# Raising the priority of the output projections' additions in VectorE's order, in a four-layer hybrid kernel on one core

## Chip, core and metric

The kernel runs on one NeuronCore of one Trainium2 chip. The metric is the device time of one execution in microseconds (us); smaller is better. A run is one timed execution; the time of a kernel is the median of its runs. Beside the timed runs one execution was recorded by the hardware profiler, and all rows of the profile come from that one.

## The reference

The reference takes a sequence of 1024 tokens of width 1024, puts 16 learned "meta" tokens in front (1040 tokens that count), and sends them through four layers. Each layer normalises the residual stream, projects it to the inputs of a mixer, runs the mixer, gates its output, projects that back to width 1024 and adds it to the residual stream:

```python
h = concat(padding, meta, x)
for i in range(4):
    u = rmsnorm(h, norm_gain[i])
    if i % 3 == 0:   y = attention_branch(u, ...)   # layers 0 and 3: sliding window, 16 heads, 4 kv heads
    elif i % 3 == 1: y = mlstm_branch(u, ...)       # layer 1: 8 heads, 128 keys, 256 values
    else:            y = hgrn2_branch(u, ...)       # layer 2: 8 heads, 128 by 128
    h = h + where(valid, y, 0)
return h[:, first_real_token:]

# the end of each branch, for instance attention
return (o * silu(z)).astype(u.dtype) @ w_out
```

The last line, the output projection, and the addition `h + y` are what the change is about. All in float32.

## The kernel before

**Layout.** The residual stream `x` stands in SBUF, transposed: 8 tiles of 128 channels (index `m`) by 1040 tokens. Tokens are worked on in three chunks of 400, 384 and 256 columns (`CHUNKS`; the last layer leaves the 16 meta tokens out and has 384, 384 and 256). Every large product is made of three matmuls, since each float32 operand is split into a high part and a remainder, `h` and `l` (`split`, lines 194 to 196: a copy on ScalarE, a subtraction on VectorE): high by high, high by low, low by high.

**Output projection** (`proj_out`, line 297). It takes two 128-row pieces of a mixer's gated output at a time (two heads' worth in attention and in the third kind of layer, one head's in the second kind) and adds their product with the output weights into `x`. For each chunk, `ysplit` (line 310) splits the two pieces into `yh` and `yl`; then for each of the 8 channel tiles `m` and the two pieces `k`, `product` (line 318) issues three matmuls into one PSUM tile `acc` (line 326). When `k` is 1 the sum is whole, and line 329 adds it on VectorE from PSUM into `x`. Below, this instruction is called an **x-addition**. There are 8 for each chunk and 480 in all: 192 in the two attention layers, 192 in the second layer, 96 in the third. After a layer's last projection `fin` runs behind each x-addition: the square of `x` on ScalarE and its addition on VectorE for the next layer's normalisation (`Norm.sq`, lines 351 and 355), or the store of the result in the last layer.

**PSUM.** All PSUM tiles, whatever they are for, come from one pool of 8 buffers of one bank each (`psum`, line 147). The names tell their use: `pj` projections (the input projections of line 231 and 281 and the output projection), `pm`, `pt`, `po`, `pa` the mixers' scores, transposes, outputs and sums. A tile is free again when the last engine has read it; for an output projection that is the x-addition.

**Order of the work.** TensorE's order is written out by hand: the body of each layer is a list of steps with costs (`[cost, function, prefetch]`), woven from the mixers' steps and filling work by their costs (`weave`, line 58), and TensorE runs what the steps issue in that very order (`manual_schedule`, line 118). The weights of a step are loaded and split some 12 us of step cost ahead (`LOOKAHEAD`, line 1503). The orders on VectorE, ScalarE, GpSimd and the DMA queue are made when the program is built: a planner goes through the program on a clock of its own, and whenever an engine is free it takes, of the instructions that are ready by that clock, the one with the smallest priority number. The number is the instruction's place in the order in which the program was written out. On the chip each engine then works through its fixed list. `hi` lowers the number by 40 places for what a function issues:

```python
PRIO = 40
def hi(fn):
    def f():
        with tc.high_priority(offset=PRIO):
            fn()
    return f
```

Before the change, `hi` is put around the mixers' steps and around `ysplit`. In attention the mixers' steps are `S_step` (line 701: scores; on VectorE the masked row minimum L734 and the reciprocal L739, on ScalarE the exponential L737, on GpSimd the scaling L740), `T_step` (line 743: TensorE transposes L755, a copy L757 and a subtraction L758) and `V_step` (line 760: product with the values L773, a copy L781 and an addition L782). One unit is one block of 128 queries for two heads. A unit's transposes come two units behind its scores, and its product with the values four units behind.

Not under `hi` are the x-additions, the rotary embedding of queries (L625 to L627), the split of queries (L528), the gates (L457, L473 to L476), the splits of weights (`wl`, L196), the normalisation of the next layer (`Norm.unit`, L373 and its split `ul`, L196) and the sums of squares (L355).

**Where output projections stand.** In layer 0 the first of the four projections is woven into the mixers (about 153 to 187 us of the profiled execution), the second too (321 to 362), and the last two form the layer's end, with the normalisation for the next layer beside them (428 to 477). Layer 3 has the same plan (2285 to 2317, 2443 to 2486, and the end of the kernel from 2546). Layer 1 has six projections between its heads (from 641 to 1328) and two at its end (1500 to 1549); layer 2 has two among its mixers (1825 to 1855, 1972 to 2003) and two at its end (2103 to 2152).

Of the kernel before, what the change touches and what calls it, by code (L numbers as in the profile page):

```python
# [12 lines left out]
ALU = mybir.AluOpType  # L13
# [100 lines left out]
def hybrid_kernel(ctx: ExitStack, tc: tile.TileContext, ins, out, layers=(0, 1, 2, 3)):  # L114
    nc = tc.nc
    v, s, g, pe, sp = nc.vector, nc.scalar, nc.gpsimd, nc.tensor, nc.sync
# [11 lines left out]
    def nm(x):  # L128
        ctr[0] += 1
        return f"{x}{ctr[0]}"  # L130
# [19 lines left out]
    def psj():  # L150
        return psum("pj", 3)
# [15 lines left out]
    x = cpool.tile([P, KT, T], F32, name="x")  # L167
# [26 lines left out]
    def split(src, h, l):  # L194
        s.copy(h, src)  # L195
        v.tensor_tensor(l, src, h.bitcast(F32), op=ALU.subtract)  # L196

    def weights(src, kind, inrow=False):
        width = src.shape[-1]
        if inrow:  # L200
            h, l = (rrow()[:, :1024] for _ in range(2))
        else:
            h = wpool.tile([P, 1024], F32R, tag="wh", name=nm("wh"), bufs=3)
            l = wpool.tile([P, 1024], F32R, tag="wl", name=nm("wl"), bufs=3)
        for z in (slice(0, width // 2), slice(width // 2, width)):
            raw = wpool.tile([P, 512], F32, tag="raw", name=nm("wr"), bufs=RAWS)[:, : width // 2]
            sp.dma_start(raw, src[:, z])
            split(raw, h[:, z], l[:, z])
        c = dict(m=128, v=256, o=512, g=272)[kind]
        return tuple(z[:, :width].rearrange("p (k c) -> p k c", c=c) for z in (h, l))  # L210
# [79 lines left out]
# [7 lines that stand above are left out]
    def proj_out(src0, src1, y, chunks=CHUNKS, fin=None, inrow=False):  # L297
        st = {}

        def pre0():  # L300
            st[0] = weights(src0, "o", inrow=inrow)

        def pre1():
            st[1] = weights(src1, "o", inrow=inrow)

        groups = []
        for n, (c0, cn) in enumerate(chunks):
            grp = []

            def ysplit(k, n=n, c0=c0, cn=cn):  # L310
                def fn():
                    yh, yl = (tpool.tile([P, 400], F32R, tag=z, name=nm(z), bufs=YS)[:, :cn] for z in ("yh", "yl"))
                    split(y(k)[:, c0 : c0 + cn], yh, yl)
                    st["y", n, k] = yh, yl

                return [0.0, hi(fn), None]

            def product(m, k, n=n, c0=c0, cn=cn):
                h, l = st[m // 4]
                mc = slice((m % 4) * P, (m % 4 + 1) * P)  # L320
                if k == 0:
                    st["p", n, m] = psj()
                acc = st["p", n, m]
                yh, yl = st["y", n, k]
                for i, (a, b) in enumerate(((h, yh), (h, yl), (l, yh))):
                    pe.matmul(acc[:, :cn], a[:, k, mc], b,  # L326
                              start=(k == 0 and i == 0), stop=(k == 1 and i == 2))
                if k == 1:
                    v.tensor_tensor(x[:, m, c0 : c0 + cn], x[:, m, c0 : c0 + cn], acc[:, :cn], op=ALU.add)  # L329
                    if fin:  # L330
                        fin(m, n, c0, cn)

            order = [(m, k) for m in range(KT - Y_LAST) for k in range(2)]
            order += [(m, k) for k in range(2) for m in range(KT - Y_LAST, KT)]
            for m, k in order:
                pre = (pre0, pre1)[m // 4] if (n == 0 and m % 4 == 0 and k == 0) else None
                grp.append([3 * cn * MM, lambda m=m, k=k, product=product: product(m, k), pre])
            groups.append(([ysplit(0), ysplit(1)], grp))
        return groups
# [1103 lines left out]
    for pos, i in enumerate(layers):  # L1443
# [3 lines left out]
        def fin(m, n, c0, cn, nxt=nxt):  # L1447
            if nxt is not None:
                nxt.sq(m, n, c0, cn)
            else:  # L1450
                lo = max(c0, NMETA)
                sp.dma_start(out[m, :, lo - NMETA : c0 + cn - NMETA], x[:, m, lo : c0 + cn])
# [169 lines left out]
```

## Time and profile before

| what | value |
|---|---|
| median of 3 runs | 2601.44 us |
| the 3 runs | 2598.78 to 2603.09 us |
| the profiled execution | 2596.91 us |
| its span, first to last instruction | 2595.1 us |
| granted TensorE clock, mean | 0.999 |
| TensorE busy | 2547.2 us, 98% |
| VectorE busy | 1960.2 us, 76% |
| ScalarE busy | 1689.9 us, 65% |
| GpSimd busy | 245.6 us, 9% |

In the profile PE is TensorE's matmuls, PEld its weight loads, DVE VectorE, ACT ScalarE and POOL GpSimd. L329 is line 329 of the kernel; a helper's line, such as L196, stands for all who call it, and is told apart by the tile that it writes. `x<-x,pj` is an instruction that writes `x` and reads `x` and `pj`. A row of the view of waits reads: who waited, on whom, us in total, how many times, the longest. A row of the timeline reads: start in us, duration in us, engine, line, operation, tiles, shapes, how many; in brackets how long the engine had been idle before it, and whose end released it. A row of the view by stretches gives the stretch and its length, then busy time of PE, PEld, DVE, ACT and POOL.

### The profile page before, as it was taken

The numbers are of one execution on the slowest core, as the hardware profiler recorded it, in microseconds if no ns is written. First come the engines' busy times: TensorE is split into PE (matmuls) and PEld (weight loads), VectorE is DVE, ScalarE is ACT, GpSimd is POOL, SyncE is SP. The second block draws the span as 40 slices with busy tenths as digits, with TensorE's granted clock in tenths as the row PEclk, the third lists the DMA queues.
The fourth block names the chain that finished last, engine by engine and source line by source line (L and its number), as shares of the span: only waits on it lengthen the run. The fifth ranks groups of instructions, "written<-read, shape, count | busy, mean of one in ns | idle before, by whom it ended". The sixth has DMA issues, their size and how long they took to land.

```text
span 2595.1 us, 54389 instructions
## 1 busy us (share of the span) xinstructions
PE 2547.2 (98%) x20446; PEld 2486.5 (96%) x20446; DVE 1960.2 (76%) x5290; ACT 1689.9 (65%) x4434; POOL 245.6 (9%) x564
## 2 busy tenths in 40 slices
PE   8999999999999999999999999999999999999999
PEld 8899999999999999999999999999999999999999
DVE  7897898775656564747474688988888978887996
ACT  8766766666464645555555757877676857767772
POOL 0321231000000000000000000010000000321330
PEclk9999999999999999999999999999999999999999
DMA  5223212021111111111111111111111113212112
GB/s 157 62 66 93 59 43 69 30 67 56 44 54 46 50 49 51 42 58 41 51 46 52 51 34 34 34 35 34 38 39 34 34 51 91 62 44 85 56 42 78
DMA packets 86058, 140.21 MB, mean 54 GB/s; under 512 B 12425, under 2 KB 39186, under 8 KB 85794
## 3 DMA queue, kind: packets, MB, share of 16 engines
q1 hardware_dynamic: 85794, 136.73, 17.1%
q8 instruction: 161, 2.64, 0.4%
q14 instruction: 103, 0.84, 0.1%
HBM read 121.83 MB, written 4.27 MB: 49 GB/s over the span
## 4 chain that ended last, share of the span: by engine, by line
PE 65%; DVE 13%; ACT 9%; issue 2%; DMA 2%; POOL 0%; SPq 0%; DVEq 0%; ACTq 0%; POOLq 0%
PE pj L231 29%; PE pj L326 15%; PE pj L281 10%; DVE wl L196 1%; ACT Sm L737 1%; PE po L1019 1%; PE po L1021 1%; PE pa L1035 1%; DVE Sm L734 1%; PE po L773 1%; ACT wh L195 1%; PE pt L755 1%; ACT X L1249 1%; PE pj L277 1%; DVE t L457 1%
## 5 line engine op out<-in xcount | busy, mean ns | idle before, releaser
L231 PE MATMUL pj<-uh,wh 128*128 128x256 f32 (+2 forms) x2688 | 914.8, 340 | 6.9 <-ACT uh L401 6.4
L231 PE MATMUL pj<-ul,wh 128*128 128x256 f32 (+2 forms) x2688 | 864.2, 322 | 0.3
L231 PE MATMUL pj<-uh,wl 128*128 128x256 f32 (+2 forms) x2688 | 864.3, 322 | 0.0
L231 PEld LDWEIGHTS pj<-uh,wh 128*128 128x128 f32 x2688 | 507.4, 189 | 16.3 <-ACT uh L401 6.4
L231 PEld LDWEIGHTS pj<-ul,wh 128*128 128x128 f32 x2688 | 507.9, 189 | 6.4 <-DVE ul L196 0.9
L231 PEld LDWEIGHTS pj<-uh,wl 128*128 128x128 f32 x2688 | 507.2, 189 | 0.0
L196 DVE TENSOR_TENSOR wl<-wr,wh 128x512 fp32r<-128x512 f32 (+1 forms) x338 | 234.7, 703 | 52.0 <-ACT wh L195 49.3
L195 ACT CAST wh<-wr 128x512 fp32r<-128x512 f32 (+1 forms) x338 | 202.9, 613 | 103.6 <-PE pj L326 32.7
L326 PE MATMUL pj<-yh,wh 128*128 128x384 f32 (+2 forms) x768 | 253.2, 330 | 9.8 <-DVE x L329 8.3
L329 DVE TENSOR_TENSOR x<-x,pj 128x384 f32<-128x384 f32 (+2 forms) x480 | 234.7, 509 | 32.8 <-PE pj L326 31.6
L326 PE MATMUL pj<-yl,wh 128*128 128x384 f32 (+2 forms) x768 | 245.8, 320 | 0.0
L326 PE MATMUL pj<-yh,wl 128*128 128x384 f32 (+2 forms) x768 | 245.8, 320 | 0.0
L281 PE MATMUL pj<-wh,uh 128*128 128x256 f32 (+1 forms) x768 | 232.7, 303 | 0.0
L281 PE MATMUL pj<-wl,uh 128*128 128x256 f32 (+1 forms) x768 | 216.4, 282 | 0.0
L281 PE MATMUL pj<-wh,ul 128*128 128x256 f32 (+1 forms) x768 | 215.9, 281 | 0.0
L737 ACT ACTIVATE Sm<-Sm,s 128x257 f32<-128x257 f32 (+2 forms) x272 | 131.1, 483 | 88.4 <-DVE s L734 85.9
L740 POOL TENSOR_TENSOR Sm<-Sm,s 128x512 f32<-128x512 f32 (+2 forms) x136 | 139.3, 1024 | 403.5 <-DVE s L739 383.3
L458 ACT ACTIVATE t<-t 128x384 f32<-128x384 f32 (+2 forms) x240 | 117.9, 491 | 76.5 <-DVE t L457 75.0
L326 PEld LDWEIGHTS pj<-yh,wh 128*128 128x128 f32 x768 | 144.5, 188 | 14.0 <-DVE x L329 10.4
L195 ACT CAST yh<-r 128x384 fp32r<-128x384 f32 (+2 forms) x120 | 57.0, 479 | 152.0 <-PE pj L326 136.3
L457 DVE SCALAR_TENSOR_TENSOR t<-pj,t 128x400 f32<-128x400 f32 (+2 forms) x168 | 86.5, 515 | 81.6 <-ACT t L456 80.3
L281 PEld LDWEIGHTS pj<-wh,uh 128*128 128x128 f32 x768 | 144.7, 188 | 2.2
(296 smaller groups left out, 5468.3 us busy)
## 6 DMA issues: line engine op xcount, KB each, us to landing
wr<-in_b_win SPq DMA_DIRECT2D x124, 256.0 KB, 2.8
wr<-in_a_win SPq DMA_DIRECT2D x80, 256.0 KB, 2.8
wr<-in_c_win SPq DMA_DIRECT2D x64, 256.0 KB, 2.8
wr<-in_a_wout SPq DMA_DIRECT2D x32, 256.0 KB, 3.0
wr<-in_b_wout SPq DMA_DIRECT2D x32, 256.0 KB, 2.7
t<-t SPq DMA_DIRECT2D x100, 48.0 KB, 1.9
cs<-in_rope SPq DMA_DIRECT2D x11, 400.0 KB, 3.6
cs<-in_rope SPq DMA_DIRECT2D x11, 384.0 KB, 3.5
```

The costliest lines, as they stand in the source:

```text
L195: s.copy(h, src)
L196: v.tensor_tensor(l, src, h.bitcast(F32), op=ALU.subtract)
L231: pe.matmul(acc[:, :cn], a[:, k, :], b[:, k, c0 : c0 + cn], start=(k == 0 and i == 0), stop=(k == KT - 1 and i == 2))
L277: pe.matmul(acc[:48, :nc], um[0][:, k, :], m[:, kk, :], start=(k == 0 and m is wh), stop=(k == KT - 1 and m is wl))
L281: pe.matmul(acc[:cn, :nc], a[:, k, c0 : c0 + cn], m[:, kk, :], start=(k == 0 and j == 0), stop=(k == KT - 1 and j == 2))
L326: pe.matmul(acc[:, :cn], a[:, k, mc], b, start=(k == 0 and i == 0), stop=(k == 1 and i == 2))
L329: v.tensor_tensor(x[:, m, c0 : c0 + cn], x[:, m, c0 : c0 + cn], acc[:, :cn], op=ALU.add)
L457: v.scalar_tensor_tensor(a[:, :cn], z, 0.0, a[:, :cn], op0=ALU.min, op1=ALU.subtract)
L458: s.activation(a[:, :cn], a[:, :cn], AF.Exp)
L734: v.tensor_tensor_reduce(Sm[:nq, u, :nk], S[:nq, u, :nk], R["masks"][:nq, P + mo : P + mo + nk], rq, sinks[u], ALU.add, ALU.min, st[:nq, u ...
L737: s.activation(Sm[:nq, u, : nk + 1], Sm[:nq, u, : nk + 1], AF.Exp, scale=-1.0, bias=st[:nq, u : u + 1], accum_out=den[:nq, u : u + 1])
L740: g.tensor_tensor(Sm[:nq, :, :nk], Sm[:nq, :, :nk], den[:nq].rearrange("p (u c) -> p u c", c=1).to_broadcast([nq, 2, nk]), op=ALU.mult)
```

## The change

Line 329 is issued under `hi`. The priority number of each of the 480 x-additions falls by 40 places. Nothing else is edited; `fin`, which follows, stays as it was. `hi` gives back a function that runs its argument with the lower number, so the call at the end of the new line runs it at once.

```diff
                 if k == 1:
-                    v.tensor_tensor(x[:, m, c0 : c0 + cn], x[:, m, c0 : c0 + cn], acc[:, :cn], op=ALU.add)
+                    xs = x[:, m, c0 : c0 + cn]
+                    hi(lambda: v.tensor_tensor(xs, xs, acc[:, :cn], op=ALU.add))()
                     if fin:
                         fin(m, n, c0, cn)
```

## Prediction

> **What bounds the kernel now.** I read the page's first part, then TensorE's waits, then the stretches in which x-additions run, then the timeline at two stalls.
>
> ```profile
> span 2595.1 us, 54389 instructions
> PE 2547.2 (98%) x20446; PEld 2486.5 (96%) x20446; DVE 1960.2 (76%) x5290; ACT 1689.9 (65%) x4434; POOL 245.6 (9%) x564
> ```
>
> TensorE is busy 98% of the span, so only its 2595.1 - 2547.2 = 47.9 us of idle time are to be had by another order of VectorE's work. The waits say how much of that hangs on x-additions.
>
> ```profile
> engine line waited for: us in total, times, longest us
> PE pt L755 <- POOL Sm L740: 10.7, 10, 2.2
> PE pj L326 <- DVE x L329: 8.3, 7, 2.2
> ...
> PE pm L726 <- DVE x L329: 1.9, 2, 1.7
> ```
>
> 8.3 + 1.9 = 10.2 us: TensorE wants a PSUM bank, for the next projection or for scores, whose x-addition has not run. By place:
>
> ```profile
> PE pj L326 <- DVE x L329: 2.1, 3, 1.6
> ...
> PE pm L726 <- DVE x L329: 1.7, 1, 1.7
> ```
> ```profile
> PE pj L326 <- DVE x L329: 4.0, 3, 1.4
> ```
> ```profile
> PE pj L326 <- DVE x L329: 2.2, 1, 2.2
> ...
> PE pj L231 <- ACT uh L195: 0.5, 1, 0.5
> ...
> PE pm L726 <- DVE x L329: 0.2, 1, 0.2
> ```
>
> These are three answers of the same view, for 153 to 362, 428 to 2160 and 2160 us to the end. Between attention's mixers TensorE loses 2.1 + 1.7 + 2.2 + 0.2 = 6.2 us; at the ends of layers 0, 1 and 2 (428 to 2160) it loses 4.0. Now how full the engines are there:
>
> ```profile
> core 0: us, PE busy (x) PEld busy (x) DVE busy (x) ACT busy (x) POOL busy (x), PEclk, DMA share, GB/s
> 153.00:187.00 34.00, 33.24 (x226) 31.87 (x225) 33.39 (x86) 18.84 (x52) 9.45 (x13) 1.00 0.13 37
> 320.00:362.00 42.00, 38.29 (x272) 36.33 (x272) 40.02 (x120) 26.16 (x86) 12.24 (x27) 1.00 0.14 44
> ...
> 1500.00:1549.00 49.00, 47.56 (x299) 46.92 (x297) 43.57 (x93) 22.13 (x46) 0.84 (x3) 1.00 0.07 22
> ...
> 1972.00:2003.00 31.00, 31.00 (x413) 29.77 (x413) 30.31 (x94) 18.76 (x54) 2.25 (x10) 1.00 0.07 22
> ...
> 2443.00:2486.00 43.00, 39.24 (x272) 37.07 (x272) 41.03 (x113) 26.40 (x79) 11.20 (x18) 1.00 0.12 38
> ```
> ```profile
> 600.00:1370.00 770.00, 770.00 (x5111) 760.73 (x5110) 466.65 (x1163) 421.38 (x991) 9.71 (x70) 1.00 0.15 48
> ```
>
> In layer 1 (600 to 1370) TensorE never rests and VectorE is 61% busy: nothing to win, and room to spare. Layer 2's second stretch (1972) has a TensorE without a gap as well. In layer 0's second stretch and layer 3's second one VectorE is 95% busy (40.02 of 42, 41.03 of 43) and TensorE 91%: there VectorE's order decides. This is how the largest stall comes about:
>
> ```profile
> 2462.14 0.55 DVE L329 TENSOR_TENSOR x<-x,pj 128x384 f32<-128x384 f32 x1
> ...
> 2464.01 0.87 DVE L528 TENSOR_TENSOR qs<-t,qs 64x256 fp32r<-64x256 f32 x2
> ...
> 2465.41 1.22 DVE L528 TENSOR_TENSOR qs<-t,qs 64x256 fp32r<-64x256 f32 x2
> 2466.65 0.55 DVE L329 TENSOR_TENSOR x<-x,pj 128x384 f32<-128x384 f32 x1
> ...
> 2467.26 0.45 PE L326 MATMUL pj<-yh,wh 128*128 128x384 f32 x1 [2.16 <-DVE x L329]
> ```
>
> Two x-additions stand 4.51 us apart, with mixers' work and the split of queries (L528, 0.87 and 1.22 us) between them; TensorE stands 2.16 us for the second.
>
> **The change part by part.** It removes and adds no instruction. No DMA, no matmul and no duration changes; only the place of 480 instructions in VectorE's list, and what the planner does after.
>
> ```profile
> L329 DVE TENSOR_TENSOR x<-x,pj 128x384 f32<-128x384 f32 (+2 forms) x480 | 234.7, 509 | 32.8 <-PE pj L326 31.6
> L734 DVE CUSTOM_DVE_ANT_0 Sm<-pm,masks,cons 128x256 f32<-128x256 f32 (+2 forms) x272 | 131.0, 510 | 6.1 <-PE pm L727 5.2
> L758 DVE TENSOR_TENSOR Pl<-pt,Ph 128x512 fp32r<-128x512 f32 (+1 forms) x136 | 89.4, 657 | 13.2 <-ACT Ph L757 11.5
> ```
>
> Each x-addition overlaps its neighbours a little: 234.7 / 480 = 0.49 us of VectorE. For these it frees a bank; L758 frees one for 89.4 / 136 = 0.66, L734 (two to a bank) for 2 x 131.0 / 272 = 0.96, and L528, rotary work, normalisation and weight splits free none. Putting the x-additions ahead therefore gives back more banks for the same VectorE time, which is my reason for a gain.
>
> *Term 1, attention's mixers.* At most the 6.2 us go. Against it: VectorE is 95% full, so what the x-addition passes comes later. A unit's scores have this much room before TensorE transposes them:
>
> ```profile
> 357.73 1.04 POOL L740 TENSOR_TENSOR Sm<-Sm,s 128x512 f32<-128x512 f32 x1 [0.87 <-DVE s L739]
> ...
> 359.96 0.60 PE L755 MATMUL pt<-ident,Sm 128*128 128x128 f32 x4
> ```
> ```profile
> 2461.98 1.14 POOL L740 TENSOR_TENSOR Sm<-Sm,s 128x512 f32<-128x512 f32 x1 [0.28 <-DVE s L739]
> ...
> 2464.50 0.60 PE L755 MATMUL pt<-ident,Sm 128*128 128x128 f32 x4
> ```
>
> 359.96 - 358.77 = 1.19 us and 2464.50 - 2463.12 = 1.38 us: two x-additions in front of L734 (0.98) fit, three (1.47) don't. Queries (L528) are split for scores yet to come. Bounds for this term: -6.2 (all stalls gone) to +5.6 (the first rival). I take -4.6, three quarters of the stalls: nearer to the gain because the two rows show room for two, and short of it because VectorE has only 2 us of idle time in each stretch to catch up with.
>
> *Term 2, the layers' ends.* At most 4.0 go. But what TensorE does next needs the normalised chunks, which VectorE makes with the time that is left, and the sum of its work is the same:
>
> ```profile
> 1546.37 0.55 DVE L329 TENSOR_TENSOR x<-x,pj 128x384 f32<-128x384 f32 x1
> ...
> 1546.97 0.39 PE L326 MATMUL pj<-yh,wh 128*128 128x256 f32 x1 [1.44 <-DVE x L329]
> ```
> ```profile
> 1566.45 1.02 DVE L196 TENSOR_TENSOR ul<-t,uh 128x384 fp32r<-128x384 f32 x2
> ...
> 1568.19 0.34 PE L231 MATMUL pj<-ul,wh 128*128 128x384 f32 x1
> ```
>
> The last split of layer 2's second chunk ends at 1567.47, and TensorE reads it at 1568.19: 0.72 us of room. Of this stall's 1.44 us only 0.7 can be kept unless the split comes earlier too. I take the same 0.7 for the end of layer 0, and nothing for the end of layer 2, where TensorE already waits 0.5 us for `uh` (quoted above). Sum -1.4, bounds -4.0 and 0.
>
> *Term 3, the rest.* Layer 1, layer 2's two stretches and the end of the kernel: 0. What hides it is TensorE's own work, 770.00 of 770 and 31.00 of 31 us. VectorE is 98% full in the latter (30.31 of 31); if each of the two projections' 48 x-additions held up layer 2's mixer uncovered by its 0.49 us, that would be 23 us, an end that I put no weight on, since 31 us without any gap show that the mixer has room. The end has no mixer beside it.
>
> Sum: -4.6 - 1.4 + 0 = **-6.0 us**. The profiled execution took 2596.91 us, 1.8 more than its span and 4.5 less than the median of 2601.44; I expect a profiled execution of about 2590.9 and a median of **2595.4 us**.
>
> **The rivals.** *Slower, the scores' chain (17%).* The x-additions and L734 wait in VectorE's list together. The two full stretches hold this many units (four L734 rows to a unit, two of them reads of the accumulator):
>
> ```profile
> 320.00:362.00 42.00, 8.83 (x41) 1.00 0.14 44
> 2443.00:2486.00 43.00, 9.64 (x40) 1.00 0.12 38
> ```
>
> 10 and 10. If each meets three x-additions more than before, it is 1.47 - 1.19 = 0.28 us beyond its room: 20 x 0.28 = +5.6 us, while the stalls on banks only move over to L755: 2607.0. It decides from three x-additions on. For it: L755's wait for L740 is the largest in the list (10.7 us). Against it: the 24 additions of a projection are about two to a unit.
>
> *Slower, VectorE held up by its own list (8%).* An x-addition moved ahead on the planner's clock can find its matmul unfinished on the chip, and all behind it stand.
>
> ```profile
> DVE x L329 <- PE pj L326: 31.6, 75, 1.2
> ```
>
> That happens 75 times now, 31.6 / 75 = 0.42 us each. If one in three of the 72 additions of three of attention's projections came to it: 24 x 0.42 = +10.1 us, 2611.5. [...]
>
> *Nothing to see (19%).* Either the stalls come back as others within a few us, since VectorE's work stays the same, or (7 of the 19) the order hardly changes: the planner may find the x-addition not ready when it picks L528, and 40 places reach only a few steps back. Time 2601.4, from -3 to +4.
>
> *All of it (10%).* The 10.2 us go and the chunks follow earlier: 2591.2.
>
> **How the numbers follow.** The forecast (46%) reaches from -9 to -3 us, at -6.0. A measurement of this kernel can tell about 0.2%, 5.2 us, from no change. Beyond -5.2 lie some 32 of the forecast's 46 and the 10 of "all of it": faster 0.42. Its other 14, the 19 of nothing and 1 of the chain's smallest cases: same 0.34. The other 16 and 8: slower 0.24. The range for 8 in 10 goes from 2590 (leaving out about 3 in 100 below) to 2609 (about 12 above, the upper part of both slower rivals).
>
> **What would show it.** Right: TensorE's waits for x L329 fall from 10.2 to under 3 us, L528 comes behind the x-additions at 2460 to 2470, and L755's wait for L740 stays within 3 us of 10.7. Term 2 is right if the stall at the end of layer 1 goes and about half comes back at L231. Wrong: L755 waits 15 us or more (the chain); VectorE idles before x L329 in 320 to 362 (its own list); or the waits for L329 stay above 7 (nothing moved). A stall in layer 1 or layer 2 would break term 3.

## The result and the profile after

The change makes the kernel slower. In five runs of each kernel on one chip, the median after is 2609.17 us (2606.53 to 2610.64) and before 2599.5 us (2598.78 to 2603.09). The ratio is **1.0037, with a 95% interval of 1.0026 to 1.0049**; the medians lie 9.7 us apart. The profiled execution of after took 2606.53 us, against 2596.91 before, 9.6 more. In the changed kernel every line behind 329 has moved down by one: the x-addition is L330, the sum of squares L356, the statistic's matmul L363.

The page of the changed kernel begins with its span, and busy time by engine:

```profile
span 2604.7 us, 54326 instructions
PE 2550.1 (98%) x20446; PEld 2488.7 (96%) x20446; DVE 1960.9 (75%) x5290; ACT 1689.1 (65%) x4434; POOL 246.2 (9%) x564
```

VectorE does the same work as before (1960.9 against 1960.2 us). TensorE idles 2604.7 - 2550.1 = 54.6 us instead of 47.9, 6.7 more, and for the same 20446 matmuls it is busy 2.9 us longer. So the loss has two kinds: more waiting, and slower matmuls. TensorE's waits in the changed kernel, as us in total, times, longest:

```profile
PE pt L756 <- POOL Sm L741: 14.1, 16, 2.2
PE pa L363 <- DVE t L356: 9.3, 3, 3.5
...
PE pj L326 <- DVE x L330: 0.9, 3, 0.4
```

The waits for x-additions have gone from 10.2 to 0.9 us, as the change would have it. In their place stands a wait that the kernel before did not have at all: L363, 9.3 us in three pieces. That is the **statistic** of the next layer's normalisation, a matmul with ones that sums the squares of `x` over the channels. It stands at the ends of layers 0, 1 and 2. VectorE at the end of layer 1, where `x` and `t` at L330 and L356 are the x-additions and the sums of squares:

```profile
1550.04 0.41 DVE L330 TENSOR_TENSOR x<-x,pj 128x256 f32<-128x256 f32 x1
...
1551.31 0.68 DVE L196 TENSOR_TENSOR wl<-wr,wh 128x512 fp32r<-128x512 f32 x1
1551.91 0.41 DVE L330 TENSOR_TENSOR x<-x,pj 128x256 f32<-128x256 f32 x1
1552.24 0.55 DVE L356 TENSOR_TENSOR t<-t,t 128x384 f32<-128x384 f32 x1
...
1553.51 0.41 DVE L330 TENSOR_TENSOR x<-x,pj 128x256 f32<-128x256 f32 x1
1553.84 0.55 DVE L356 TENSOR_TENSOR t<-t,t 128x384 f32<-128x384 f32 x1
```

and TensorE at the same place:

```profile
1551.27 0.28 PE L326 MATMUL pj<-yh,wl 128*128 128x256 f32 x1
1554.44 1.65 PE L363 MATMUL pa<-t,ones 128*128 128x384 f32 x2 [2.90 <-DVE t L356]
...
1556.22 0.54 PE L231 MATMUL pj<-ul,wh 128*128 128x400 f32 x1
...
1558.03 0.34 PE L231 MATMUL pj<-ul,wh 128*128 128x400 f32 x1
```

The widths tell the chunks apart. The x-additions here are 256 wide, of the last chunk; the sums of squares are 384 wide, of the middle one, and belong to x-additions that ran earlier. All of the middle chunk's sums must be there for the statistic. From 1550.04 on, five raised x-additions of the last chunk (the first, the third and the fifth are quoted) and splits of weights (`wl`) run while its last three sums (the first and the third quoted) are still to come; the third ends at 1554.39. In TensorE's hand-written order the statistic stands directly behind the end's last projection (1551.27), so TensorE idles 2.90 us. In the kernel before, TensorE takes it with no wait, and what follows is faster (the first row is VectorE's, the middle chunk's last sum):

```profile
1547.63 0.55 DVE L355 TENSOR_TENSOR t<-t,t 128x384 f32<-128x384 f32 x1
...
1548.37 0.28 PE L326 MATMUL pj<-yh,wl 128*128 128x256 f32 x1
1548.48 0.81 PE L362 MATMUL pa<-t,ones 128*128 128x384 f32 x2
...
1549.32 0.34 PE L231 MATMUL pj<-ul,wh 128*128 128x400 f32 x1
```

The same `pj<-ul,wh` takes 0.34 us before and 0.54 after the idle time (two rows of it stand in the fence of after, 0.54 and then 0.34). The view by stretches gives the reason, in the column PEclk, the third number from the end:

```profile
1550.94:1554.35 3.41, 0.60 (x6) 0.40 (x4) 3.41 (x9) 2.13 (x6) 0.00 (x0) 1.00 0.50 150
1554.35:1557.76 3.41, 3.32 (x8) 2.69 (x9) 3.06 (x8) 2.70 (x7) 0.00 (x0) 0.50 0.28 90
1557.76:1564.00 6.24, 6.24 (x44) 6.18 (x44) 5.63 (x20) 3.09 (x12) 0.00 (x0) 1.00 0.14 42
...
2158.51:2165.34 6.83, 6.19 (x17) 5.52 (x18) 6.83 (x18) 4.39 (x10) 0.00 (x0) 0.50 0.35 113
```

After the idle time the granted clock is 0.50 for 3.41 us, then 1.00 again. At the end of layer 2 it is 0.50 for twice as long. TensorE works for 3.32 of the first 3.41 us at half clock; half of that, 1.66 us, is lost, which fits the 1.67 of the tables below.

TensorE's order is the same in both kernels, so the same matmul can be looked up in both traces, and the difference of its starts says how far behind the changed kernel is at that point. (Starts in us; the last two columns belong to two experiments below, both of them the changed kernel with idle matmuls ahead of the statistic, 11 and 4.)

| matmul, start before | start after | after - before | 11 idle matmuls | 4 idle matmuls |
|---|---|---|---|---|
| last layer-0 projection, 473.01 | 473.34 | +0.33 | +1.79 | +0.78 |
| behind the x-addition stall, 475.13 | 474.16 | -0.97 | +0.49 | -0.52 |
| statistic, 476.66 | 479.29 | +2.62 | +4.08 | +3.08 |
| 486.07 | 490.34 | +4.27 | +4.19 | +4.59 |
| last layer-1 projection, 1545.02 | 1549.61 | +4.59 | +4.01 | +4.47 |
| behind the x-addition stall, 1546.97 | 1549.96 | +2.99 | +2.41 | +2.87 |
| statistic, 1548.48 | 1554.44 | +5.96 | +5.29 | +5.75 |
| 1556.18 | 1563.82 | +7.63 | +5.40 | +7.42 |
| last layer-2 projection, 2148.02 | 2154.00 | +5.98 | +2.45 | +4.44 |
| behind the x-addition stall, 2150.66 | 2154.95 | +4.29 | +0.75 | +2.75 |
| statistic, 2151.84 | 2159.15 | +7.31 | +3.78 | +5.77 |
| 2172.10 | 2182.35 | +10.25 | +3.86 | +7.40 |
| 2178.04 | 2186.34 | +8.30 | +1.90 | +5.44 |
| behind the last full stretch, 2500.10 | 2509.75 | +9.64 | +4.63 | +8.84 |

The steps of the third column, summed by kind:

| what | us |
|---|---|
| x-addition stalls at the three ends, gone | -1.30 - 1.60 - 1.69 = -4.59 |
| waits of the statistic, new | 3.59 + 2.97 + 3.02 = +9.58 |
| half clock behind these waits | 1.65 + 1.67 + 2.94 = +6.26 |
| waits for `uh` behind the end of layer 2 and what stands around them, gone | -1.95 |
| layers 0 and 3 outside the ends | 0.33 + 1.34 = +1.67 |
| layers 1 and 2 outside the ends | 0.32 - 1.65 = -1.33 |
| sum | +9.64 |

Of the 9.58 us of new waits, 4.59 are only the old stalls in a new place; the other 4.99 come from sums that are later than before.

Now the mixers of the attention layers. TensorE's waits from 153 to 362 us, and from 2160 us to the end, in the changed kernel:

```profile
PE pt L756 <- POOL Sm L741: 1.5, 3, 0.9
PE pj L326 <- DVE r L783: 1.5, 1, 1.5
...
PE pj L326 <- DVE x L330: 0.3, 1, 0.3
```
```profile
PE pt L756 <- POOL Sm L741: 4.8, 5, 2.2
...
PE pj L326 <- DVE yl L196: 1.5, 1, 1.5
...
PE pj L326 <- DVE x L330: 0.6, 2, 0.4
```

The 6.2 us that x-additions cost there are down to 0.9. But others have come: in the first stretch 1.5 us for `r` (the mixer's output, added up on VectorE) and 1.5 for the scaled scores; in the second 1.5 for `yl` (the split of that output for the next projection), in place of 1.0 for `r`, and 4.8 for the scaled scores, where before it was 2.9. How `yl` comes to be late:

```profile
2467.17 0.82 ACT L195 CAST yh<-r 128x384 fp32r<-128x384 f32 x2
...
2467.95 0.68 DVE L759 TENSOR_TENSOR Pl<-pt,Ph 128x512 fp32r<-128x512 f32 x1
2468.66 0.42 DVE L783 TENSOR_TENSOR r<-r,po 64x256 f32<-64x256 f32 x1
2469.11 0.56 DVE L196 TENSOR_TENSOR yl<-r,yh 128x384 fp32r<-128x384 f32 x1
...
2469.72 0.44 PE L326 MATMUL pj<-yl,wh 128*128 128x384 f32 x1 [1.54 <-DVE yl L196]
```

`yh` is done at 2467.99, but `yl` is made at 2469.11, behind a transposes' remainder (L759) and an addition (L783). VectorE is at work the whole time. In the kernel before the stall of this projection was for a bank; now it is for the projection's own input.

### The profile page after: what moved, and what is told of

It is laid out like the page before. It is cut to its first block, busy times and chain, and to the rows that moved or that the text cites. A ratio compares the mean times of both kernels' runs of the same rounds, so it can differ in the third digit from the quotient of the medians.

```text
span 2604.7 us, 54326 instructions
## 1 busy us (share of the span) xinstructions
PE 2550.1 (98%) x20446; PEld 2488.7 (96%) x20446; DVE 1960.9 (75%) x5290; ACT 1689.1 (65%) x4434; POOL 246.2 (9%) x564
## 3 DMA queue, kind: packets, MB, share of 16 engines
HBM read 121.83 MB, written 4.27 MB: 48 GB/s over the span
## 4 chain that ended last, share of the span: by engine, by line
PE 66%; DVE 13%; ACT 8%; DMA 2%; issue 2%; SPq 0%; POOL 0%; DVEq 0%; ACTq 0%; POOLq 0%
PE pj L231 30%; PE pj L326 14%; PE pj L281 10%; DVE wl L196 1%; PE po L1020 1%; PE po L1022 1%; ACT Sm L738 1%; PE pa L1036 1%; PE po L774 1%; DVE Sm L735 1%; PE pt L756 1%; DVE x L330 1%; PE pj L277 1%; ACT X L1250 1%; DVE Pl L759 1%
## 5 line engine op out<-in xcount | busy, mean ns | idle before, releaser
L231 PE MATMUL pj<-uh,wh 128*128 128x256 f32 (+2 forms) x2688 | 915.9, 341 | 6.6 <-ACT uh L402 6.6
L231 PE MATMUL pj<-ul,wh 128*128 128x256 f32 (+2 forms) x2688 | 864.5, 322 | 0.0
L231 PE MATMUL pj<-uh,wl 128*128 128x256 f32 (+2 forms) x2688 | 864.4, 322 | 0.0
L231 PEld LDWEIGHTS pj<-uh,wh 128*128 128x128 f32 x2688 | 508.3, 189 | 16.0 <-ACT uh L402 6.6
L231 PEld LDWEIGHTS pj<-ul,wh 128*128 128x128 f32 x2688 | 508.6, 189 | 6.1 <-issue 0.6
L231 PEld LDWEIGHTS pj<-uh,wl 128*128 128x128 f32 x2688 | 507.5, 189 | 0.0
L330 DVE TENSOR_TENSOR x<-x,pj 128x384 f32<-128x384 f32 (+2 forms) x480 | 235.5, 508 | 34.9 <-PE pj L326 32.9
L281 PE MATMUL pj<-wh,uh 128*128 128x256 f32 (+1 forms) x768 | 232.7, 303 | 0.0
L281 PE MATMUL pj<-wl,uh 128*128 128x256 f32 (+1 forms) x768 | 216.3, 282 | 0.0
L281 PE MATMUL pj<-wh,ul 128*128 128x256 f32 (+1 forms) x768 | 215.9, 281 | 0.0
L326 PEld LDWEIGHTS pj<-yl,wh 128*128 128x128 f32 x768 | 144.6, 188 | 2.4 <-DVE yl L196 2.1
L281 PEld LDWEIGHTS pj<-wh,uh 128*128 128x128 f32 x768 | 144.7, 188 | 2.2
```

The lines of the kernel that those rows point to most:

```text
L231: pe.matmul(acc[:, :cn], a[:, k, :], b[:, k, c0 : c0 + cn], start=(k == 0 and i == 0), stop=(k == KT - 1 and i == 2))
L281: pe.matmul(acc[:cn, :nc], a[:, k, c0 : c0 + cn], m[:, kk, :], start=(k == 0 and j == 0), stop=(k == KT - 1 and j == 2))
L326: pe.matmul(acc[:, :cn], a[:, k, mc], b, start=(k == 0 and i == 0), stop=(k == 1 and i == 2))
L330: hi(lambda: v.tensor_tensor(xs, xs, acc[:, :cn], op=ALU.add))()
```

## The experiments

The ratios below are to the kernel before. The first four kernels ran together (before: median 2599.3 us of 26 runs), the other four together (2599.93 us of 30 runs). The edits are shown against the changed kernel, save in the control. The changed kernel itself was not run again beside them: where a text says how far a kernel is from it, its 2609.17 us stand beside 2599.5 of the kernel before.

**1. Raised among the mixers alone.** At the ends of the layers (where `fin` is given, or the weights go in by rows) the x-additions keep their old priority.

```diff
-                    hi(lambda: v.tensor_tensor(xs, xs, acc[:, :cn], op=ALU.add))()
+                    add = lambda: v.tensor_tensor(xs, xs, acc[:, :cn], op=ALU.add)
+                    (add if inrow or fin else hi(add))()
```

> x-additions are raised only in the projections among the mixers, not in the two at each layer's end. Theory A (the loss is made at the layers' ends, where raised x-additions pass the sums of squares that TensorE's statistic waits for): the three waits of the statistic for the sums (9.3 us in the changed kernel) are gone, the three waits for x-additions at the ends (4.0 us) are back, and the time is +0 to +2 us against the kernel before, since the mixers' stretches of the changed kernel came out 2 us longer. Theory B (the scores' chain among the mixers is what costs): +7 us or more, as in the changed kernel.

Measured: 2601.19 us, ratio 1.0008 (0.9999 to 1.0017). Its waits of the transposes and for x-additions:

```profile
PE pt L757 <- POOL Sm L742: 13.4, 15, 2.2
...
PE pj L326 <- DVE x L330: 5.0, 6, 1.4
```

The wait of the statistic is not among its waits. The rise among the mixers costs 1.9 us at the median, which its interval doesn't tell from nothing; it wins nothing, though 10.2 - 5.0 = 5.2 us of stalls on x-additions are gone. L757's wait for the scores, 10.7 before, is 13.4 here and 14.1 in the changed kernel.

**2. Raised at the ends alone.**

```diff
-                    hi(lambda: v.tensor_tensor(xs, xs, acc[:, :cn], op=ALU.add))()
+                    add = lambda: v.tensor_tensor(xs, xs, acc[:, :cn], op=ALU.add)
+                    (hi(add) if inrow or fin else add)()
```

> x-additions are raised only in the two projections at each layer's end. Theory A: the three waits of the statistic for the sums stand as in the changed kernel, 2.9 to 3.5 us each, and the time is +8 to +10 us against the kernel before. Theory B: the mixers are as before, so the time is that of the kernel before, or some 4 us less since the waits for x-additions at the ends go: -4 to +1 us.

Measured: 2608.53 us, ratio 1.0036 (1.0024 to 1.0049), the whole loss.

```profile
PE pt L757 <- POOL Sm L742: 10.0, 9, 2.7
PE pa L364 <- DVE t L357: 9.2, 3, 3.5
```

The statistic waits 9.2 us, as in the changed kernel, and the scores' wait stays at 10.0. So the loss is made at the layers' ends.

**3. The squares raised as well.** `fin` runs under `hi`, so that the squares and their sums get the same 40 places.

```diff
                     if fin:
-                        fin(m, n, c0, cn)
+                        hi(lambda: fin(m, n, c0, cn))()
```

> As the changed kernel, and the squares and their sums that follow each x-addition (and the stores of the last layer) get the same priority. Theory A: the sums keep their place beside the x-additions, the waits of the statistic for them fall from 9.3 to under 3 us, the clock stays at full speed behind them, and the time falls by 8 us or more against the changed kernel: -3 to +2 us against the kernel before. What may come instead is TensorE waiting for the normalised chunks (uh, ul), which are now passed by both. A rival (VectorE's work at the ends is full, so any order costs the same): the waits move over to uh and ul and the time stays at +7 to +10 us.

Measured: 2604.81 us, ratio 1.0023 (1.0014 to 1.0033): 4.4 us better than the changed kernel, and 5.5 worse than before.

```profile
PE pa L363 <- DVE t L356: 5.8, 3, 2.2
```

The wait falls from 9.3 to 5.8 us, not below 3 as was expected. Its last sums at the end of layer 1 on VectorE:

```profile
1552.39 0.57 DVE L196 TENSOR_TENSOR ul<-t,uh 128x400 fp32r<-128x400 f32 x1 [0.27 <-ACT uh L195]
...
1553.45 0.50 DVE L356 TENSOR_TENSOR v<-v,t 128x256 f32<-128x256 f32 x1
1553.88 0.54 DVE L356 TENSOR_TENSOR t<-t,t 128x384 f32<-128x384 f32 x1
```

Now the split of the first chunk (`ul`, 400 wide) stands ahead of the last sums, and it waited for its copy on ScalarE; even a sum of the last chunk (`v`, 256 wide) runs ahead of the middle chunk's last one (`t`, 384 wide). The order among equals is the planner's, by its clock. To raise both brings back less than half of the loss. A part of what it wins is the clock: behind this end's wait of 1.91 us it stays at 1.00 (last section).

**4. Idle matmuls ahead of the statistic.** The changed kernel, with 11 matmuls of ones by ones into the statistic's bank, which the statistic then overwrites. They need nothing from VectorE, so they fill the gap and end no wait.

```diff
                 st = psa()
+                if n == 1:
+                    for _ in range(11):
+                        pe.matmul(st[:, :P], ones, ones, start=True, stop=True)
                 pe.matmul(st[:, :cn], ones, self.acc[n], start=True, stop=True)
```

> As the changed kernel, with 11 small matmuls of ones by ones put ahead of the statistic of the middle chunk, into its own PSUM bank, where TensorE stands idle for 2.9 to 3.5 us at three layers' ends; their result is overwritten. Theory C (part of the loss, some 5 us, is the granted clock of 0.50 in the first microseconds after those waits): the clock stays at 1.00 behind them, the waits get no longer than the time the filler takes away, and the time falls by 3 to 5 us against the changed kernel: +5 to +7 us against the kernel before. If the slow matmuls behind the wait are slow for another reason: the time is that of the changed kernel, +9 to +11 us.

Measured: 2601.78 us, ratio 1.0011 (1.0002 to 1.002), 7.4 us below the changed kernel at the median (3 to 5 were expected), and 2604.7 - 2599.7 = 5.0 us by the profiled spans. The end of layer 1, and the clock behind it:

```profile
1550.80 2.62 PE L365 MATMUL pa<-ones 128*128 128x128 f32 x22
1553.77 0.91 PE L366 MATMUL pa<-t,ones 128*128 128x384 f32 x2 [0.35 <-DVE t L356]
```
```profile
1554.20:1556.20 2.00, 2.00 (x12) 1.87 (x11) 1.99 (x6) 1.82 (x4) 0.00 (x0) 1.00 0.27 82
```

The statistic is as late as in the changed kernel: in the table of starts it steps by 3.59, 2.88 and 3.03 us in this kernel, and by 3.59, 2.97 and 3.02 in the changed one. What goes is what follows: 0.11, 0.11 and 0.08 us in place of 1.65, 1.67 and 2.94. The filling does no useful work; it keeps the granted clock at 1.00 behind these three waits. Elsewhere in this trace the clock was halved all the same: at 403.38, behind a wait of 2.09 us, where the changed kernel kept 1.00 behind one of 2.07. That is where the 1.79 us in the first row of the table come from.

**5. The statistic later in TensorE's order.** The middle chunk's statistic, with the normalisation that hangs on it, is placed 3 us later among the next layer's first projections.

```diff
-NORM_AT = (4000.0, 0.7), (5000.0, 0.5), (8000.0, 0.5)
+NORM_AT = (4000.0, 0.7), (8000.0, 0.5), (8000.0, 0.5)
```

> The changed kernel with the middle chunk's statistic and its normalisation placed 3 us later in TensorE's order (8000 for 5000). Theory A (the loss is made where the statistic waits for sums of squares that the raised x-additions passed): its three waits fall from 9.3 us to under 1.5, the half clock behind them goes, nothing of that comes back at L231, and the time is 9 to 13 us below the changed kernel's, 2596 to 2600. Rival D (VectorE simply has too much to do at the layers' ends, wherever the statistic stands): 5 us or more come back as waits for uh and ul at L231, and the time stays at 2604 or above.

Measured: 2602.33 us, ratio 1.0007 (0.9998 to 1.0015), 6.8 us below the changed kernel: less than the 9 to 13 expected. TensorE no longer waits for the statistic. But:

```profile
PE pj L231 <- ACT uh L195: 2.0, 3, 1.0
PE pj L231 <- DVE ul L196: 1.7, 5, 0.5
```

2.0 + 1.7 = 3.7 us stand here as waits for the normalised chunks, where the kernel before had 0.5 (for `uh`): 3.2 us have come back. The middle chunk of layer 2's end is among them:

```profile
1570.76 0.44 PE L231 MATMUL pj<-uh,wh 128*128 128x384 f32 x1 [1.01 <-ACT uh L195]
...
1573.28 0.41 PE L281 MATMUL pj<-wh,ul 128*128 128x256 f32 x1
...
1575.90 0.28 PE L281 MATMUL pj<-wh,uh 128*128 128x256 f32 x1
```

and behind this gap of 1.01 us and one of 0.41 at 1571.61, L281 takes 0.41 us until 1575.6, where it falls to 0.31 and 0.28: half clock again (the mean over 1571 to 1575 is 0.66). So both theories hold a part: the statistic's place makes most of the loss, and of the 4.0 us of stalls that the change takes away here, most come back at the next thing that VectorE has to deliver.

**6. The control.** The kernel before, with the same 3 us.

> The control: the kernel before with the statistic placed 3 us later in the same way. Theory A: the statistic did not wait there, so nothing is won or lost, within 2 us of the kernel before. If it wins over 3 us, the place of the statistic was a cost of its own, and the run above says less.

Measured: 2600.03 us, ratio 1.0003 (0.9994 to 1.0011). The place of the statistic costs nothing where x-additions are not raised.

**7. Fewer idle matmuls.** As experiment 4, with 4 in place of 11.

```diff
-                    for _ in range(11):
+                    for _ in range(4):
```

> The changed kernel with 4 in place of 11 idle matmuls ahead of the middle chunk's statistic, some 0.9 us of work in each of the three gaps of about 3 us, so that 2.0 to 2.6 us of idle time are left in each. If it is a gap of nearly 3 us that halves the granted clock and 2 us are short enough, the clock stays at 1.00 behind the gaps, and the time is that of the kernel with 11 (2601 to 2603). If 2 us of idle time halve it as well, the time is the changed kernel's (2606 to 2609).

Measured: 2607.15 us, ratio 1.003 (1.0018 to 1.0041), all but as slow as the changed kernel and 5.4 us slower than with 11.

```profile
1551.26 1.05 PE L365 MATMUL pa<-ones 128*128 128x128 f32 x8
1554.23 1.39 PE L366 MATMUL pa<-t,ones 128*128 128x384 f32 x2 [1.92 <-DVE t L356]
```
```profile
1555.20:1557.20 2.00, 2.00 (x7) 1.78 (x6) 1.64 (x5) 1.87 (x5) 0.00 (x0) 0.50 0.39 130
```

1.92 us of idle time, the shortest of the three gaps that were left, are enough here for a granted clock of 0.50. At the layers' ends nothing else differs from 11 idle matmuls: the statistic steps by 3.60, 2.88 and 3.02 us, but behind it 1.51, 1.67 and 1.63 us are lost where there it was 0.11, 0.11 and 0.08.

**8. Raised at the ends alone, and the statistic later.** Experiments 2 and 5 together, the version that the others made look best.

> x-additions raised at the layers' ends alone, and the statistic 3 us later. Theory A: the 4.0 us of x-addition stalls at the ends go, the statistic no longer waits, the mixers keep their order: 2 to 4 us faster than the kernel before, 2595 to 2597. Rival D: 2604 or above, with waits for uh and ul. If it comes out at the kernel before's time, the 4.0 us come back at another wait, as point two of the prediction supposed for half of them.

Measured: 2599.95 us, ratio 1.0002 (0.9993 to 1.001). It does not beat the kernel before, as 2595 to 2597 would have: the waits at L231 are there as in experiment 5, 2.0 us for `uh` and 1.6 for `ul`.

No version of these eight is faster than the kernel before.

## Why the prediction was wrong

**What bounds the kernel: right.** The stalls on x-additions were real, 10.2 us, and the change takes them down to 0.9.

**Term 2, the layers' ends: the step that failed.** The prediction had -1.4 us, with bounds of -4.0 and 0; it came to -4.59 + 9.58 + 6.26 - 1.95 = +9.3. The reasoning began well: what VectorE makes for the next layer comes out of the time that is left, and the sum of its work is the same. Then it looked at one such product, the normalised chunks at L231 (0.72 us of room), and left out the one that TensorE wants first. Between the last projection and L231 stands the statistic, with no step between it and the projection, and its input is made by just the instructions that the x-additions pass, the sums of squares, which the diff leaves at their old priority. The rows were there to be read: in the kernel before, the statistic starts at 1548.48, directly behind the projection's last matmul (1548.37), and the last of its sums is done at 1548.18. That is 0.30 us of room: by these rows, most of a stall of 1.44 us that goes would come back right there, even with the sums on time. The bound at 0 was wrong for the same reason: no row said that an end could not lose.

The second half of this miss is the clock. The prediction counted a wait as its own length. The rows that it quoted show a clock of 1.00 throughout, but the trace of the kernel before has two stretches at 0.50 elsewhere: from 1622.79 us, behind a wait of 2.10, and from 2093.83, behind one of 1.91, each for 3.41 us. Experiments 4 and 7 measure the price of the waits in question: 0.3 us in all with 11 idle matmuls, 4.8 us with 4, and 6.3 in the changed kernel, while the statistic comes 9.5 to 9.6 us late in all three. The length of a gap doesn't tell by itself what follows: the changed kernel's gap of 2.90 us at the end of layer 1 and the one of 1.92 in experiment 7 were followed by 0.50, the changed kernel's one of 2.07 before 401.99 us by 1.00 (last section).

**Term 1, attention's mixers: wrong in sign, small.** Predicted -4.6, measured +1.7 in the trace (0.33 in layer 0, 1.34 in layer 3) and +1.9 us at the median in experiment 1, which is not told from nothing. The stalls on x-additions did go, 6.2 to 0.9 us, though the split of queries (now L529) does not stand behind the x-additions from 2460 to 2470, as foretold: it still runs between them (2461.69, 2465.35). But giving back banks sooner was worth nothing, because the projection that gets the bank then waits for `r` (1.5) or `yl` (1.5), or the transposes for their scores. This is read from the trace's waits; no run tried them one by one. The prediction's list of things that could be late had the scores alone. Its row on the scores' room was right in kind: L756's wait grew from 10.7 to 14.1, 3.4 us, a little over the 3 that it allowed and under the 15 at which it would have called the scores' chain the winner.

**Term 3: nearly right.** Layer 1 has +0.32 and layer 2's mixers -1.65, against 0. Layer 2's gain is no merit of the change, it is the clock: in the kernel before, these 3.41 us behind a wait of 1.91 us for `kT` (the mixer's transposed keys) run at 0.50.

```profile
2093.83:2097.24 3.41, 3.41 (x14) 3.41 (x12) 2.28 (x5) 1.65 (x3) 0.00 (x0) 0.50 0.46 146
```

The changed kernel waits 1.90 us at the same matmul, and its clock stays at 1.00; over these matmuls it falls from 7.5 us behind to 6.0.

**The rivals.** The scores' chain is a part of the small loss among the mixers, not of the result. VectorE was not held up by its own list: its idle time before x-additions is 32.9 us, 76 times, against 31.6 and 75, and none of it lies in 320 to 362.

```profile
DVE x L330 <- PE pj L326: 32.9, 76, 1.2
```

The loss came by none of the rivals. The nearest in kind was the first case of "nothing to see", stalls that come back as others: it is what experiments 1, 5 and 8 show, at 1.0008, 1.0007 and 1.0002. The range ended at 2609, set by the rivals' own prices, and the result is 0.2 us above it.

**What stays open.** Which of VectorE's instructions would have to go for the 10.2 us to be won wasn't tried; each experiment moves work, none takes VectorE's away. There is one trace of each kernel, and which waits the clock answers changes from trace to trace (behind the wait for `kT`, 1.91 us before and 1.90 after, it was 0.50 and 1.00), so a difference of 1.7 us at one place between two traces can be the clock's alone.

## What to carry to other kernels

When an engine that is nearly full gets a new order, list everything that the bound engine takes from it behind the stall, in the bound engine's own order, beginning with the very next instruction, and give each its room; what the raised work passes shows up at the first of them without room. Where the producer has no slack, removing a stall moves it. Count a new wait of some two us on TensorE at more than its length, since the matmuls behind it may run at half the clock (at the end of layer 1 in experiment 7, 1.92 us of idle time were followed by 0.50 for 3.41 us, and 1.67 us more were lost); before a fixed wait that can't be moved, idle matmuls that fill it can be worth more than they cost (11 of them were; 4 left gaps of 1.92 us and more, and won 2.0 us in place of 7.4).

## What the runs showed of the hardware

**Half the clock behind an idle TensorE, for 3.41 us at a time, in these ten traces.** In them, the end of the kernel aside, the granted clock falls to 0.50 for 3.41 us, and three times for 6.83, as at the end of layer 2 in the changed kernel, which explains the 2.94 us there. In the changed kernel's trace the starts lie whole multiples of 3.4133 us apart: behind the one at 479.15, those at 1554.35, 1629.44 and 2158.51 come after 1075.20, 1150.29 and 1679.36 us, 315, 337 and 492 of them; in the kernel before, 2093.83 - 1622.79 = 471.04 us is 138. Below, a stretch is the 3.41 us between two neighbouring points of this grid, and a border is such a point.

**In these traces the idle time within one such stretch told the cases apart better than the length of the gap.** At the end of layer 1, the first row is experiment 7, the other two are experiment 3:

```profile
1551.12:1554.53 3.41, 1.49 (x12) 1.30 (x11) 3.30 (x9) 2.27 (x6) 0.00 (x0) 1.00 0.49 153
```
```profile
1549.81:1553.22 3.41, 2.76 (x24) 2.56 (x22) 3.14 (x8) 3.41 (x10) 0.73 (x2) 1.00 0.00 0
1553.22:1556.63 3.41, 2.15 (x10) 1.89 (x11) 3.41 (x9) 1.75 (x5) 0.46 (x1) 1.00 0.15 37
```

In experiment 7 the gap of 1.92 us lies within one stretch (3.41 - 1.49 = 1.92), and the next is at 0.50. In experiment 3 a border at 1553.22 cuts the gap of 1.91 us in two, 0.65 and 1.26 us, and the clock stays at 1.00 until 1560. In the changed kernel, too, gaps of 2.07 us before 401.99 and 2.25 us before 2217.00, cut into parts of at most 1.34 and 1.79 us, left it at 1.00:

```profile
404.00:408.00 4.00, 4.00 (x26) 3.96 (x25) 3.94 (x10) 2.93 (x8) 2.29 (x2) 1.00 0.06 14
...
2219.00:2223.00 4.00, 3.29 (x26) 3.12 (x25) 3.49 (x16) 3.41 (x12) 1.62 (x3) 1.00 0.03 7
```

Even a gap of 2.87 us at the end of layer 2 in experiment 2, cut into 1.80 and 1.07, did. Counted over the ten traces (17 to 2590 us), the next stretch was at 0.50 behind all 38 full-clock stretches with 1.90 us or more of idle TensorE, behind 4 of the 19 with 1.70 to 1.90, 6 of the 182 with 0.60 to 1.70, and none of the 7259 with less. What decided the ten below 1.90 us is open; in experiment 5, waits of 0.25, 1.01 and 0.41 us in one stretch, 1.67 together, were enough.
